# The output row of token 0 of a Fourier mixer: from a weighted row sum on VectorE to products with one stationary column, and a weight unit moved behind the copies

## The chip, the cores and the metric

The kernel runs on one core of a Trainium2 chip. A core has TensorE (PE, the matmul engine, with a loader for its stationary operand, PEld), VectorE (DVE), ScalarE (ACT), GpSimd (POOL) and SyncE (SP), each with a program of its own that it works through in order, and DMA engines that move data between memory and the core. The metric is the time of one execution on the device, in microseconds (us).

## The reference, cut to what matters

An encoder of two layers, for 512 tokens of 1024 channels. Layer 0 mixes with attention and a recurrent branch, layer 1 with a Fourier transform; after each mixer comes a SwiGLU FFN of 2816 hidden channels, and every part is normed before and after. The change is in the Fourier mixer:

```python
def fourier_mixer(h, w):
    B, S, D = h.shape
    g = h.astype(jnp.float32).reshape(B, S, FOURIER_GROUPS, FOURIER_GROUP_DIM)
    f = jnp.fft.fft2(g, axes=(1, 3), norm='ortho').real
    return f.reshape(B, S, D).astype(h.dtype) @ w

def reference(...):
    for l in range(DEPTH):
        hn = rmsnorm(x, ln_mix_pre[l])
        ...
            m = fourier_mixer(hn, w_fourier_out[l // 2])
        x = x + rmsnorm(m, ln_mix_post[l])
        hn = rmsnorm(x, ln_ffn_pre[l])
        x = x + rmsnorm(swiglu(hn, w_ffn_gate[l], w_ffn_up[l], w_ffn_down[l]), ln_ffn_post[l])
```

The real part of the transform is symmetric in the frequencies: it is the sum of a part E that is even and a part T that is odd, so two output rows come from one pair, as E + T and E − T.

## The kernel before, in words

**Products.** Each float32 operand is split into a high part and the rest (`split`: a cast on ACT at L104, a subtraction on DVE at L107), and `mm3` makes three products of the parts (L110 to L112).

**Weights.** They come in units of two halves of 512 KB. `prep_half` loads a half into one of three `raw` buffers (SP, L177 or L179), ACT makes `whi` of it and DVE `wlo`. A load has to wait until the `wlo` three halves earlier is done, and since ACT and DVE work in program order, the place where `prep_one` is called sets where the two halves stand in their queues. `next_unit` preps some units ahead; in the Fourier stage the calls of `prep_one` are written out by hand.

**The Fourier stage**, between the two FFNs. `pre_norm_tok` norms a token tile t into `hnhi` and `hnlo`. `pos_dft` and `pos_rest` transform over the positions (PE, out tile `put`; `take_u` splits it into `u`), `ch_dft` and `ch_rest` over the channels of each of the four groups g (out `pe` and `po`, split into `feo`). The linear map by w_fourier_out uses the folded weights `wfold` (sums and differences of rows j and 256 − j, written to memory by `fold_w` during the first FFN): `map_part(i, h, g)` accumulates, for 128 tokens i and 512 output channels h, the even part in `psm[i][0][h]` and the odd part T in `psm[i][1][h]`. The tile of tokens i=1 goes first. `map_rest` adds the rows that have no partner (channel 128 of each group, one more for the ends): `fr` with the weight tile `wr`.

**The row at token 0.** T is zero there, and its row in `psm[0][1][h]` takes the map of column 256 of the transforms instead, the partner of column 0. Before the change this row is summed on DVE: four `raw` loads of wfold (L1040), `acc` (L1042 to L1045) with the column values `e256` as scalars, split into `acch` and `accl`, and put into the row by two products with a one-hot column, L1064.

**Out of the map.** `map_out(i)` copies T to `yt` (ACT, L1070), makes the sum and the difference `y` (DVE, L1074), and norms: times gain (L297), sums of squares (ACT, L298), `m` and `r` (DVE L249 and L250, POOL L251), new `x` (L307), squares of x (ACT, L257), `xn` (L279). `turn_x` transposes xn on PE (`pT`, L287), ACT and DVE split it into `hnhi` and `hnlo` of the last FFN, whose first products are `pc` (L110 to L112 with 256 columns while only two tiles are there).

Of the kernel before, what the change touches and what calls it, by code (L numbers as in the profile page):

```python
# [10 lines left out]
F32 = mybir.dt.float32  # L11
F32R = mybir.dt.float32r
# [4 lines left out]
P = 128  # L17
D = 1024
# [17 lines left out]
def encoder_kernel(  # L36
# [27 lines left out]
    def tile1k(name, dtype=F32):  # L64
        return tiles.tile([P, 1024], dtype, name=nm(name), tag="t")
# [12 lines left out]
    def f(ap):  # L78
        return ap.bitcast(F32)
# [20 lines left out]

    def split(hi, lo, src, hi_eng=A, lo_eng=V):

        if hi_eng is A:
            A.copy(hi, src)  # L104
        else:
            hi_eng.tensor_copy(hi, src)
        lo_eng.tensor_tensor(out=lo, in0=src, in1=f(hi), op=ALU.subtract)  # L107

    def mm3(ps, l, r, start, stop, **kw):
        T.matmul(ps, lhsT=l[0], rhs=r[0], start=start, stop=False, **kw)  # L110
# [54 lines left out]
    emitted = [0]  # L165
    consumed = [0]

    def prep_half():
        i = emitted[0]
        if i >= len(units):  # L170
            return
        kind, ap = units[i]
        halves = prepped.setdefault(i, [])
        h = len(halves)
        raw = raws.tile([P, 1024], F32, name=nm("raw"), tag="raw")
        if kind == "c":
            nc.sync.dma_start(raw.rearrange("p (k c) -> p k c", c=256), ap[:, 4 * h:4 * h + 4, :])  # L177
        elif kind == "r":
            nc.sync.dma_start(raw, ap[:, h, :])  # L179
        else:  # L180
            nc.sync.dma_start(raw.rearrange("p (dh j) -> p dh j", j=P),
                              (lru_w_a, lru_w_i)[h].rearrange("d h i j -> i (d h) j"))
        hi, lo = tile1k("whi", F32R), tile1k("wlo", F32R)
        split(hi, lo, raw, hi_eng=V if i in HI_DVE else A, lo_eng=G if i in LO_POOL else V)
        halves.append((hi, lo))
        if h:
            emitted[0] += 1
# [13 lines left out]
    def fold_w(g):  # L201

        a, b, c = (tile1k("fold") for _ in range(3))
        nc.sync.dma_start(a, w_fourier_out[g * 256:g * 256 + P, :])
        gather(b, w_fourier_out, rowx["w%d" % g])
        G.memset(b[0:1, :], 0.0)
        V.tensor_tensor(out=c, in0=a, in1=b, op=ALU.add)
        V.tensor_tensor(out=a, in0=a, in1=b, op=ALU.subtract)
        for z, w in enumerate((c, a)):
            G.dma_start(wfold[g * 256 + z * P:g * 256 + (z + 1) * P, :], w)  # L210

    def prep_one():
        prep_half()
        prep_half()

    last_unit = [len(units)]

# [661 lines left out]
    def chw(i):  # L879
        return chT[i // 8][:, (i % 8) * P:(i % 8 + 1) * P]  # L880

    def load_ch():
        chT.extend(tile1k("ch", F32R) for _ in range(2))
        for z in range(2):
            for n in range(2):
                G.dma_start(chw(2 * z + n), dft_ch[n, :, z * 256:z * 256 + P])
        G.memset(f(chT[0][:, S:]), 0.0)
        G.memset(f(chT[1]), 0.0)
        for g in range(4):
            G.dma_start(chw(4 + g)[g:g + 1, :], dft_ch[0, 0:1, 512:512 + P])  # L890
# [3 lines left out]
        G.memset(f(chw(13)[:, 0:1]), 1.0)


    last_row = []

    def load_last():
        w128 = tile1k("w128")  # L900
        G.memset(w128, 0.0)
        for q in range(3):
            G.dma_start(w128[32 * q:32 * q + 4, :], w_fourier_out.rearrange("(g j) d -> g j d", j=256)[:, P, :])
        last_row.append(w128)

    posT = []
    calls = [0]
# [21 lines left out]
                posT[k].append(w)  # L929

    last_unit[0] = len(units) - 4 - NF // 2 * 3
    ffn(0, after0, 6, load_dft, early=lambda u: fold_w(u - 1) if 0 < u < 5 else None)
    last_unit[0] = len(units)
    load_last()
    prep_one()


# [37 lines left out]
        take_u(g)  # L975

    prep_one()
    w128, = last_row

    feo = hpool.tile([P, 16, 256], F32R, name=nm("feo"), tag="hnhi")  # L980
    rows_ = hpool.tile([P, 4, D], F32R, name=nm("rows"), tag="hnlo")
    acch, accl, wr, fr = rows_[:, 0, :], rows_[:, 1, :], rows_[:, 2, :], rows_[:, 3, 0:256]


    fe, fo, e256 = [None] * 4, [None] * 4, {}

    def ch_dft(g):
        pe, po = bank("pe"), bank("po")
        ut, ur = uts[g], uts["r"]
        mm3(pe[:, 0:258], (chw(0), chw(1)), [a[:, 0:258] for a in ut], True, False)  # L990
        for a in ur:
            T.matmul(pe[:, 0:258], lhsT=chw(4 + g)[0:4, :], rhs=a[0:4, 0:258], start=False, stop=a is ur[1])
        mm3(po[:, 0:256], (chw(2), chw(3)), [a[:, 256:512] for a in ut], True, True)
        eo = feo[:, 4 * g:4 * g + 4, :]
        e, o = fe[g], fo[g] = (eo[:, 0, :], eo[:, 1, :]), (eo[:, 2, :], eo[:, 3, :])
        split(*e, pe[:, 0:256])
        e256[g] = sm("e256")
        V.tensor_copy(e256[g], pe[:, 256:257])
        for a in o:
            G.memset(f(a[:, 0:1]), 0.0)  # L1000
        split(*[a[:, 1:256] for a in o], po[:, 1:256])

    def ch_rest():
        ps = bank("pe")
        n = 0
        for g in (0, 1, 2, 3, "r"):
            for a in uts[g]:
                k = 4 if g == "r" else P
                T.matmul(ps[:, 0:258], lhsT=chw(12 if g == "r" else 8 + g)[0:k, :], rhs=a[0:k, 0:258], start=n == 0, stop=n == 9)
                n += 1  # L1010
        e256["r"] = sm("e256")
        V.tensor_copy(e256["r"], ps[:, 256:257])
        c = A.copy(fr[:, 0:256], ps[:, 0:256])
        v = V.tensor_tensor(out=fr[64:P, 0:256], in0=ps[64:P, 0:256], in1=f(fr[64:P, 0:256]), op=ALU.subtract)
        order_after(A.copy(wr, w128), [c])
        order_after(V.tensor_tensor(out=wr[32:64, :], in0=w128[32:64, :], in1=f(wr[32:64, :]), op=ALU.subtract), [v])

    for g in range(4):
        ch_dft(g)
# [13 lines left out]
    wf = [next_unit(-1) for g in range(4)]  # L1033
    prep_one()


    acc = tile1k("acc")
    for g in range(4):
        raw = raws.tile([P, 1024], F32, name=nm("raw"), tag="raw")
        nc.sync.dma_start(raw, wfold[g * 256:g * 256 + P, :])  # L1040
        if g:
            V.scalar_tensor_tensor(out=acc, in0=raw, scalar=e256[g], in1=acc, op0=ALU.mult, op1=ALU.add)  # L1042
        else:
            V.tensor_scalar(out=acc, in0=raw, scalar1=e256[0], scalar2=None, op0=ALU.mult)
    V.scalar_tensor_tensor(out=acc[0:32, :], in0=w128[0:32, :], scalar=e256["r"][0:32, :], in1=acc[0:32, :], op0=ALU.mult, op1=ALU.add)  # L1045
    split(acch, accl, acc)
    prep_one()

    psm = [[[bank("pm"), bank("pm")] for _ in range(2)] for _ in range(2)]

    def map_part(i, h, g):
        sl = slice(i * P, (i + 1) * P)
        d = slice(h * S, (h + 1) * S)
        ps = psm[i]
        mm3(ps[0][h], [a[:, sl] for a in fe[g]], [a[:, d] for a in wf[g][0]], g == 0, False)
        mm3(ps[1][h], [a[:, sl] for a in fo[g]], [a[:, d] for a in wf[g][1]], g == 0, g == 3 and i == 1)

# [108 lines left out]
```

## Time and profile before

| what | value |
|---|---|
| median of 3 runs | 1036.85 us (1035.66 to 1037.36) |
| the profiled execution | 1037.44 us, span 1035.7 us, mean granted clock 0.984 |
| PE busy | 1001.8 us (97% of the span) |
| DVE busy | 500.7 us (48%) |
| ACT busy | 377.9 us (36%) |
| POOL busy | 115.4 us (11%) |

Times in the trace count from the start of the span; the Fourier stage lies from about 594 to 655 us. The busy share of PE is a mean over the whole program, and where a short stretch has another limit it does not show there. Idle time of an engine matters only if the work that ends last waits for it.

### The profile page before, as it was taken

The numbers are of one execution on the slowest core, as the hardware profiler recorded it, in microseconds if no ns is written. First come the engines' busy times: TensorE is split into PE (matmuls) and PEld (weight loads), VectorE is DVE, ScalarE is ACT, GpSimd is POOL, SyncE is SP. The second block draws the span as 40 slices with busy tenths as digits, with TensorE's granted clock in tenths as the row PEclk, the third lists the DMA queues.
The fourth block names the chain that finished last, engine by engine and source line by source line (L and its number), as shares of the span: only waits on it lengthen the run. The fifth ranks groups of instructions, "written<-read, shape, count | busy, mean of one in ns | idle before, by whom it ended". The sixth has DMA issues, their size and how long they took to land.

```text
span 1035.7 us, 12334 instructions
## 1 busy us (share of the span) xinstructions
PE 1001.8 (97%) x4877; PEld 835.4 (81%) x4877; DVE 500.7 (48%) x765; ACT 377.9 (36%) x621; POOL 115.4 (11%) x196
## 2 busy tenths in 40 slices
PE   8999999999999999999999997699999999999996
PEld 7887677789888888888888886698888888888885
DVE  6869988753554222223323688726422232343304
ACT  5378567643333211232213464515311322233201
POOL 1056111111020000005130130100000000000001
PEclk8999999999999999999999999799999999999998
DMA  6424212412776432223442067017622233124002
GB/s 219 130 84 142 93 41 82 144 40 83 240 271 204 136 104 82 82 82 79 136 122 82 3 212 235 21 42 220 186 82 82 81 120 104 61 95 129 1 1 81
DMA packets 79797, 114.78 MB, mean 111 GB/s; under 512 B 6466, under 2 KB 66415, under 8 KB 79740
## 3 DMA queue, kind: packets, MB, share of 16 engines
q1 hardware_dynamic: 70858, 97.16, 29.7%
q0 software_dynamic: 8592, 16.32, 5.2%
q8 instruction: 38, 0.62, 0.3%
q10 hardware_dynamic: 290, 0.53, 0.1%
q14 instruction: 19, 0.16, 0.0%
HBM read 106.65 MB, written 7.34 MB: 110 GB/s over the span
## 4 chain that ended last, share of the span: by engine, by line
PE 82%; DVE 9%; issue 3%; DMA 2%; ACT 2%; POOL 1%; SPq 0%; DVEq 0%; POOLq 0%; ACTq 0%
PE pc L112 15%; PE pc L111 15%; PE pc L110 15%; PE pj L112 9%; PE pj L111 9%; PE pj L110 9%; DVE wlo L107 2%; DVE p L630 2%; DVE p L636 1%; DMA raw<-wfold 1%; PE pT L287 1%; DMA raw<-in_w_in_dram 1%; DVE aT L107 1%; PE pqk L110 1%; ACT whi L104 1%
## 5 line engine op out<-in xcount | busy, mean ns | idle before, releaser
L107 DVE TENSOR_TENSOR wlo<-raw,whi 128x1024 fp32r<-128x1024 f32 x170 | 207.0, 1239 | 206.7 <-ACT whi L104 173.8
L112 PE MATMUL pc<-hnhi,wlo 128*128 128x512 f32 (+1 forms) x784 | 288.2, 368 | 2.6 <-DVE wlo L107 2.6
L111 PE MATMUL pc<-hnlo,whi 128*128 128x512 f32 (+1 forms) x784 | 288.5, 369 | 0.0
L110 PE MATMUL pc<-hnhi,whi 128*128 128x512 f32 (+1 forms) x784 | 287.4, 369 | 1.1 <-ACT whi L104 0.6
L104 ACT CAST whi<-raw 128x1024 fp32r<-128x1024 f32 x164 | 167.9, 1049 | 108.7 <-DMA raw<-in_w_ffn_gate_dram 47.6
L112 PEld LDWEIGHTS pc<-hnhi,wlo 128*128 128x128 f32 x784 | 148.5, 189 | 27.2 <-DVE wlo L107 3.1
L110 PEld LDWEIGHTS pc<-hnhi,whi 128*128 128x128 f32 x784 | 147.7, 189 | 26.4 <-ACT hnhi L104 1.2
L111 PEld LDWEIGHTS pc<-hnlo,whi 128*128 128x128 f32 x784 | 148.6, 189 | 24.7 <-DVE hnlo L107 0.4
L110 PE MATMUL pj<-whi,gs 128*128 128x512 f32 x352 | 136.9, 389 | 0.0
L112 PE MATMUL pj<-whi,gs 128*128 128x512 f32 x352 | 136.9, 389 | 0.0
L111 PE MATMUL pj<-wlo,gs 128*128 128x512 f32 x352 | 136.9, 389 | 0.0
L94 ACT ACTIVATE gated<-pc 128x512 f32<-128x512 f32 x44 | 26.1, 597 | 242.8 <-PE pc L112 242.8
L797 DVE TENSOR_TENSOR gated<-gated,pc 128x512 f32<-128x512 f32 x44 | 30.1, 686 | 111.9 <-PE pc L112 111.7
L112 PEld LDWEIGHTS pj<-whi,gs 128*128 128x128 f32 x352 | 66.1, 188 | 13.8
L110 PEld LDWEIGHTS pj<-whi,gs 128*128 128x128 f32 x352 | 66.1, 188 | 13.8
L111 PEld LDWEIGHTS pj<-wlo,gs 128*128 128x128 f32 x352 | 66.1, 188 | 13.5
L251 POOL TENSOR_TENSOR r<-m,mhalf 128x1 f32<-128x1 f32 x32 | 19.2, 599 | 497.4 <-DVE m L250 456.1
L107 DVE TENSOR_TENSOR gs<-gated,gs 128x512 fp32r<-128x512 f32 x44 | 28.8, 688 | 74.7 <-ACT gs L104 74.6
L104 ACT CAST gs<-gated 128x512 fp32r<-128x512 f32 x44 | 25.5, 619 | 100.5 <-PE pj L111 53.2
L298 ACT ACTIVATE junk<-pj 128x512 f32<-128x512 f32 x24 | 14.3, 597 | 75.0 <-DVE y L297 53.9
L297 DVE TENSOR_TENSOR y<-pj,gpost 128x512 f32<-128x512 f32 x24 | 16.4, 686 | 48.7 <-PE pj L112 48.7
L94 ACT ACTIVATE p<-p,mn 128x512 f32<-128x512 f32 x32 | 23.0, 719 | 25.8 <-DVE mn L630 24.3
(255 smaller groups left out, 1217.1 us busy)
## 6 DMA issues: line engine op xcount, KB each, us to landing
raw<-in_w_ffn_gate_dram SPq DMA_DIRECT2D x44, 512.0 KB, 4.2
raw<-in_w_ffn_up_dram SPq DMA_DIRECT2D x44, 512.0 KB, 4.9
raw<-in_w_ffn_down_dram SPq DMA_DIRECT2D x44, 512.0 KB, 3.4
raw<-in_w_in_dram SPq DMA_DIRECT2D x20, 512.0 KB, 4.4
raw<-wfold SPq DMA_DIRECT2D x12, 512.0 KB, 4.4
raw<-in_w_mix_out_dram SPq DMA_DIRECT2D x8, 512.0 KB, 3.4
wfold<-fold POOLq DMA_DIRECT2D x8, 512.0 KB, 3.3
fold<-in_w_fourier_out_dram SPq DMA_DIRECT2D x4, 512.0 KB, 6.7
```

The lines of the kernel that those rows point to most:

```text
L94: ins = A.activation(out_, in_, func, **kw)
L104: A.copy(hi, src)
L107: lo_eng.tensor_tensor(out=lo, in0=src, in1=f(hi), op=ALU.subtract)
L110: T.matmul(ps, lhsT=l[0], rhs=r[0], start=start, stop=False, **kw)
L111: T.matmul(ps, lhsT=l[0], rhs=r[1], start=False, stop=False, **kw)
L112: T.matmul(ps, lhsT=l[1], rhs=r[0], start=False, stop=stop, **kw)
L251: G.tensor_tensor(out=r, in0=m, in1=mhalf[:, 0:1], op=ALU.pow)
L287: T.transpose(pt[:, k * P:(k + 1) * P], xh[:, k * P:(k + 1) * P], ident)
L297: V.tensor_tensor(out=ys[h], in0=ps[h], in1=g[:, h * S:(h + 1) * S], op=ALU.mult)
L298: sq[0] = A.activation(junk, ps[h], AF.Square, scale=RD, accum_out=ss[h])
L630: last_score[0] = V.tensor_tensor_reduce(out=pr[m], in0=ps[m], in1=bias[h][:, 384 - t * P:384 - t * P + S], op0=ALU.add, op1=ALU.min, scal ...
L797: V.tensor_tensor(out=gated[fc], in0=gated[fc], in1=ps, op=ALU.mult)
```

## The change

In the Fourier stage, the row at token 0 is made on PE: `map_row(h)` accumulates into partition 0 of `psm[0][1][h]` 13 products with one stationary column (the column 256 of the transforms, held as high and low part in `ends`, four columns for the four groups, and one column of `fr`), each with 512 moving columns. The DVE sum `acc`, its four loads, its split and the L1064 products go. The weight tile `wr` is made by `fold_last` in the first FFN (u=5), written to memory as `wlast` and loaded once by POOL. `prep_one` of the second unit moves from before the map into `map_out(1)`, behind the copies of T, and its casts are ordered after the last copy.

```diff
     def split(hi, lo, src, hi_eng=A, lo_eng=V):
 
-        if hi_eng is A:
-            A.copy(hi, src)
-        else:
-            hi_eng.tensor_copy(hi, src)
+        c = A.copy(hi, src) if hi_eng is A else hi_eng.tensor_copy(hi, src)
         lo_eng.tensor_tensor(out=lo, in0=src, in1=f(hi), op=ALU.subtract)
+        return c
...
-        split(hi, lo, raw, hi_eng=V if i in HI_DVE else A, lo_eng=G if i in LO_POOL else V)
+        order_after(split(hi, lo, raw, hi_eng=V if i in HI_DVE else A, lo_eng=G if i in LO_POOL else V), after)
...
+    def fold_last():
+
+        a, b = tile1k("fold"), tile1k("fold", F32R)
+        G.memset(a, 0.0)
+        for q in range(3):
+            nc.sync.dma_start(a[32 * q:32 * q + 4, :], w_fourier_out.rearrange("(g j) d -> g j d", j=256)[:, P, :])
+        A.copy(b, a)
+        V.tensor_tensor(out=b[32:64, :], in0=a[32:64, :], in1=f(b[32:64, :]), op=ALU.subtract)
+        G.dma_start(wlast, f(b))
...
-    ffn(0, after0, 6, load_dft, early=lambda u: fold_w(u - 1) if 0 < u < 5 else None)
+    ffn(0, after0, 6, load_dft, early=lambda u: fold_w(u - 1) if 0 < u < 5 else fold_last() if u == 5 else None)
     last_unit[0] = len(units)
-    load_last()
     prep_one()
...
-    acch, accl, wr, fr = rows_[:, 0, :], rows_[:, 1, :], rows_[:, 2, :], rows_[:, 3, 0:256]
+    wr, fr = rows_[:, 0, :], rows_[:, 1, 0:258]
+
+    ends = rows_[:, 2, 0:4], rows_[:, 2, 4:8]
+    G.dma_start(f(wr), wlast)
...
-        e256[g] = sm("e256")
-        V.tensor_copy(e256[g], pe[:, 256:257])
+        split(*[a[:, g:g + 1] for a in ends], pe[:, 256:257])
...
-    prep_one()
-
-
-    acc = tile1k("acc")
-    for g in range(4):
-        raw = raws.tile([P, 1024], F32, name=nm("raw"), tag="raw")
-        nc.sync.dma_start(raw, wfold[g * 256:g * 256 + P, :])
...
-    split(acch, accl, acc)
     prep_one()
...
         T.matmul(psm[i][0][h], lhsT=fr[:, sl], rhs=wr[:, d], start=False, stop=True)
-        if i == 0:
-            for a in (acch, accl):
-                T.matmul(psm[i][1][h], lhsT=chw(13), rhs=a[:, d], start=False, stop=a is accl)
+
+    def map_row(h):
+
+        d = slice(h * S, (h + 1) * S)
+        row = psm[0][1][h][0:1, :]
+        T.matmul(row, lhsT=fr[:, 256:257], rhs=wr[:, d], start=False, stop=False)
+        for g in range(4):
+            mm3(row, [a[:, g:g + 1] for a in ends], [a[:, d] for a in wf[g][0]], False, False)
...
         for h in range(2):
-            A.copy(ts[h], psm[i][1][h])
+            copied[0] = A.copy(ts[h], psm[i][1][h])
...
+        if i:
+            prep_one(copied)
...
+                if g == 3 and i == 0:
+                    map_row(h)
                 map_part(i, h, g)
```

The lines of the changed kernel lie elsewhere (a cast of `split` is L103, its subtraction L104, mm3 L108 to L110, the y of map_out L1060). DVE in the map, before: `acc` is the row sum, the `rows` tile its low part, and the two `wlo` around it those of the second unit (up).

```order
L107 TENSOR_TENSOR wlo_5214<-raw_5211,whi_5213 128x1024
L1044 TENSOR_SCALAR acc_5217<-raw_5218,e_839_5098 128x1024
L1042 SCALAR_TENSOR_TENSOR acc_5217<-raw_5221,e_842_5116,acc_5217 128x1024
L1042 SCALAR_TENSOR_TENSOR acc_5217<-raw_5224,e_845_5134,acc_5217 128x1024
L1042 SCALAR_TENSOR_TENSOR acc_5217<-raw_5227,e_848_5152,acc_5217 128x1024
L1045 SCALAR_TENSOR_TENSOR acc_5217<-w_810_4925,e_850_5169,acc_5217 32x1024
L107 TENSOR_TENSOR wlo_5236<-raw_5233,whi_5235 128x1024
L107 TENSOR_TENSOR rows_5085<-acc_5217,rows_5085 128x1024
L107 TENSOR_TENSOR wlo_5242<-raw_5239,whi_5241 128x1024
L1074 TENSOR_TENSOR y_5304<-pm_5249,yt_5303 128x512
L1074 TENSOR_TENSOR y_5304<-pm_5250,yt_5303 128x512
L297 TENSOR_TENSOR y_5309<-y_5304,gpost_5177 128x512 x2
```

The same place in the changed kernel, from the first y on (the row ahead of it is the wlo of the second gate half):

```order
L1060 TENSOR_TENSOR y_5277<-pm_5222,yt_5276 128x512
L1060 TENSOR_TENSOR y_5277<-pm_5223,yt_5276 128x512
L306 TENSOR_TENSOR y_5282<-y_5277,gpost_5178 128x512 x2
L1060 TENSOR_TENSOR yt_5276<-pm_5222,yt_5276 128x512
L1060 TENSOR_TENSOR yt_5276<-pm_5223,yt_5276 128x512
L306 TENSOR_TENSOR y_5291<-yt_5276,gpost_5178 128x512 x2
L104 TENSOR_TENSOR wlo_5301<-raw_5298,whi_5300 128x1024
L258 TENSOR_SCALAR m_5310<-ss_5283 128x1
L259 TENSOR_TENSOR m_5311<-ss_5284,m_5310 128x1
L258 TENSOR_SCALAR m_5318<-ss_5292 128x1
L104 TENSOR_TENSOR wlo_5307<-raw_5304,whi_5306 128x1024
L316 SCALAR_TENSOR_TENSOR x_82<-y_5282,r_5312,x_82 128x512 x2
```

The five acc rows and the split of acc are gone, and the two wlo of up stand now behind the y products, one ahead of the `m` and one ahead of the first `x`.

DVE at the end of the norm of token tile 3, before (`w` is the folded input; `hnlo` the low part that the transform over positions reads; the two wlo are the halves of the first wfold unit):

```order
L853 TENSOR_TENSOR w_4916<-h_4914 128x4x127
L854 TENSOR_TENSOR w_4916<-h_4914 128x4x127
L107 TENSOR_TENSOR wlo_4933<-raw_4930,whi_4932 128x1024
L860 SCALAR_TENSOR_TENSOR hnlo_4689<-w_4916,r_4910,hnhi_4688 128x512 x2
L107 TENSOR_TENSOR wlo_4939<-raw_4936,whi_4938 128x1024
L107 TENSOR_TENSOR u_5033<-put_5020,u_5033 4x258
```

and after:

```order
L862 TENSOR_TENSOR w_4925<-h_4923 128x4x127
L863 TENSOR_TENSOR w_4925<-h_4923 128x4x127
L104 TENSOR_TENSOR wlo_4937<-raw_4934,whi_4936 128x1024
L104 TENSOR_TENSOR wlo_4943<-raw_4940,whi_4942 128x1024
L869 SCALAR_TENSOR_TENSOR hnlo_4698<-w_4925,r_4919,hnhi_4697 128x512 x2
L104 TENSOR_TENSOR u_5037<-put_5024,u_5037 4x258
```

The second wlo stands ahead of the hnlo pair instead of behind it.

PE at the last group of the map for i=0 in the changed kernel (`pm` are the accumulators, `rows` the stationary columns of `ends` or `fr`, `feo` the transform of the tokens):

```order
L108 MATMUL pm_5221<-whi_5190,feo_5088 128x512
L109 MATMUL pm_5221<-wlo_5191,feo_5088 128x512
L110 MATMUL pm_5221<-whi_5190,feo_5088 128x512
L1048 MATMUL pm_5220<-rows_5089 1x512
L108 MATMUL pm_5220<-whi_4936,rows_5089 1x512
L109 MATMUL pm_5220<-wlo_4937,rows_5089 1x512
L110 MATMUL pm_5220<-whi_4936,rows_5089 1x512
L108 MATMUL pm_5220<-whi_5078,rows_5089 1x512
L109 MATMUL pm_5220<-wlo_5079,rows_5089 1x512
L110 MATMUL pm_5220<-whi_5078,rows_5089 1x512
```

Before, none of the 1x512 rows is there, and the map ends with these:

```order
L110 MATMUL pm_5248<-whi_5201,feo_5084 128x512
L111 MATMUL pm_5248<-wlo_5202,feo_5084 128x512
L112 MATMUL pm_5248<-whi_5201,feo_5084 128x512
L1061 MATMUL pm_5245<-rows_5085 128x512
L1064 MATMUL pm_5247<-rows_5085,ch_4063 128x512 x2
L1061 MATMUL pm_5246<-rows_5085 128x512
L1064 MATMUL pm_5248<-rows_5085,ch_4063 128x512 x2
L287 MATMUL pT_5423<-ident,xn_5341 128x128 x4
```

Thirteen products with one stationary column come ahead of the last group of each h, and the pairs of L1064 go.

## Rows read from the trace of the kernel before

**Rows 1.** Waits of PE: engine, line, releaser; us in total, times, longest.

```profile
PE pT L287 <- ACT yt L1070: 11.7, 1, 11.7
...
PE pc L112 <- DVE wlo L107: 2.6, 1, 2.6
```

**Rows 2.** The chain that ended last, 605 to 690 us: start, us, what.

```profile
630.60 3.17 DMA raw<-wfold
633.86 1.29 DVE acc L1042
635.17 4.63 DMA raw<-in_w_ffn_up_dram
```

**Rows 3.** Timeline of PE: start, us, line, out<-in, stationary shape, output, count [idle before].

```profile
606.84 0.28 PE L110 MATMUL put<-pos,hnhi 128*4 128x258 f32 x1
...
608.01 0.28 PE L111 MATMUL put<-pos,hnhi 128*4 128x258 f32 x1
...
608.37 0.28 PE L112 MATMUL put<-pos,hnlo 128*128 128x258 f32 x1
```

**Rows 4.** Timeline of DVE at the same place.

```profile
607.02 1.41 DVE L860 SCALAR_TENSOR_TENSOR hnlo<-w,r,hnhi 128x512 fp32r<-128x512 f32 x2
608.57 1.23 DVE L107 TENSOR_TENSOR wlo<-raw,whi 128x1024 fp32r<-128x1024 f32 x1
```

**Rows 5.** Timeline of PE, the map of i=0 and the transposes.

```profile
629.52 0.39 PE L110 MATMUL pm<-whi,feo 128*128 128x512 f32 x1
...
640.18 0.39 PE L112 MATMUL pm<-whi,feo 128*128 128x512 f32 x1
...
641.31 0.61 PE L1064 MATMUL pm<-rows,ch 128*128 128x512 f32 x2
653.60 1.94 PE L287 MATMUL pT<-ident,xn 128*128 128x128 f32 x8 [11.67 <-ACT yt L1070]
```

**Rows 6.** Timeline of DVE, from the last gate half to the next unit.

```profile
629.35 1.23 DVE L107 TENSOR_TENSOR wlo<-raw,whi 128x1024 fp32r<-128x1024 f32 x1 [1.74 <-ACT whi L104]
...
642.25 1.29 DVE L1074 TENSOR_TENSOR y<-pm,yt 128x512 f32<-128x512 f32 x2
...
648.15 1.41 DVE L307 SCALAR_TENSOR_TENSOR x<-y,r,x 128x512 f32<-128x512 f32 x2 [0.62 <-POOL r L251]
...
656.44 1.94 DVE L107 TENSOR_TENSOR hnlo<-pT,hnhi 128x512 fp32r<-128x512 f32 x3
658.52 0.69 DVE L107 TENSOR_TENSOR hnlo<-pT,hnhi 128x512 fp32r<-128x512 f32 x1 [0.15 <-ACT hnhi L104]
...
659.73 1.28 DVE L297 TENSOR_TENSOR y<-y,gpost 128x512 f32<-128x512 f32 x2
...
673.23 2.36 DVE L107 TENSOR_TENSOR wlo<-raw,whi 128x1024 fp32r<-128x1024 f32 x2
```

**Rows 7.** Timeline of ACT: a weight cast, the copies of i=0, the hnhi casts.

```profile
607.50 1.04 ACT L104 CAST whi<-raw 128x1024 fp32r<-128x1024 f32 x1
...
652.43 1.05 ACT L1070 COPY yt<-pm 128x512 f32<-128x512 f32 x2
...
657.91 0.58 ACT L104 CAST hnhi<-pT 128x512 fp32r<-128x512 f32 x1 [0.26 <-PE pT L287]
...
671.54 1.07 ACT L104 CAST hnhi<-pT 128x512 fp32r<-128x512 f32 x2 [0.32 <-PE pT L287]
```

**Rows 8.** Timeline of PE in the last FFN: the later transposes, the wait for wlo.

```profile
670.90 1.04 PE L287 MATMUL pT<-ident,xn 128*128 128x128 f32 x8
674.51 0.39 PE L112 MATMUL pc<-hnhi,wlo 128*128 128x256 f32 x1 [2.57 <-DVE wlo L107]
```

**Rows 9.** Busy time by stretch: PE, PEld, DVE, ACT, POOL, PE clock, DMA share, GB/s.

```profile
350.00:420.00 70.00, 70.00 (x311) 57.98 (x310) 18.29 (x18) 16.54 (x20) 0.00 (x0) 1.00 0.30 90
...
670.00:674.50 4.50, 1.62 (x12) 1.38 (x12) 3.73 (x8) 2.29 (x4) 0.55 (x1) 1.00 0.00 0
674.50:678.50 4.00, 3.99 (x20) 3.99 (x21) 2.29 (x3) 0.00 (x0) 0.00 (x0) 0.57 0.70 196
```

More of the change, by code (lines that the diff above doesn't have):

```diff
@@ L159, in encoder_kernel @@
     wfold = dram.tile([D, D], F32, name="wfold")
+    wlast = dram.tile([P, D], F32, name="wlast")
     for u in range(4):
@@ L166, in encoder_kernel, with prep_half @@
     consumed = [0]
-    def prep_half():
+    def prep_half(after=()):
         i = emitted[0]
@@ L210, in fold_w, with prep_one @@
             G.dma_start(wfold[g * 256 + z * P:g * 256 + (z + 1) * P, :], w)
-    def prep_one():
-        prep_half()
-        prep_half()
+    def fold_last():
[6 more added lines that the diff above has]
+        G.dma_start(wlast, f(b))
+    def prep_one(after=()):
+        prep_half(after)
+        prep_half(after)
     last_unit = [len(units)]
@@ L893, in load_ch @@
             G.dma_start(chw(12)[g:g + 1, g:g + 65:32], dft_ch[0, 0:1, 0:3])
[L894 to L904, printed above, removed]
     posT = []
@@ L977, in encoder_kernel @@
     prep_one()
-    w128, = last_row
     feo = hpool.tile([P, 16, 256], F32R, name=nm("feo"), tag="hnhi")
     rows_ = hpool.tile([P, 4, D], F32R, name=nm("rows"), tag="hnlo")
-    acch, accl, wr, fr = rows_[:, 0, :], rows_[:, 1, :], rows_[:, 2, :], rows_[:, 3, 0:256]
-    fe, fo, e256 = [None] * 4, [None] * 4, {}
+    wr, fr = rows_[:, 0, :], rows_[:, 1, 0:258]
+    ends = rows_[:, 2, 0:4], rows_[:, 2, 4:8]
+    G.dma_start(f(wr), wlast)
+    fe, fo = [None] * 4, [None] * 4
     def ch_dft(g):
@@ L1010, in ch_rest @@
                 n += 1
[L1011 to L1016, printed above, removed]
+        A.copy(fr, ps[:, 0:258])
+        V.tensor_tensor(out=fr[64:P, :], in0=ps[64:P, 0:258], in1=f(fr[64:P, :]), op=ALU.subtract)
     for g in range(4):
@@ L1034, in encoder_kernel @@
     prep_one()
-    acc = tile1k("acc")
-    for g in range(4):
-        raw = raws.tile([P, 1024], F32, name=nm("raw"), tag="raw")
-        nc.sync.dma_start(raw, wfold[g * 256:g * 256 + P, :])
[L1041 to L1045, printed above, removed]
-    split(acch, accl, acc)
-    prep_one()
     psm = [[[bank("pm"), bank("pm")] for _ in range(2)] for _ in range(2)]
@@ L1055, in map_part @@
         mm3(ps[0][h], [a[:, sl] for a in fe[g]], [a[:, d] for a in wf[g][0]], g == 0, False)
-        mm3(ps[1][h], [a[:, sl] for a in fo[g]], [a[:, d] for a in wf[g][1]], g == 0, g == 3 and i == 1)
+        mm3(ps[1][h], [a[:, sl] for a in fo[g]], [a[:, d] for a in wf[g][1]], g == 0, g == 3)
     def map_rest(i, h):
@@ L1080, in map_out @@
             pre_norm(t, g_fpre1, after=sq[0])
+    copied = [None]
     for i in (1, 0):
```

## The prediction, made before the changed kernel ran

> **What bounds the kernel now.** I read the waits of TensorE (PE) first, because nothing can be gained where PE never waits. After the start of the program there is one long entry: the transposes pT at L287, the first work of the last FFN, wait 11.7 us, put down to ACT's yt at L1070. Behind it stand 2.6 us of pc L112 on a wlo of VectorE (DVE) [rows 1]. Everything the change touches lies just in front of these.
>
> The chain of waits says who is late. Around 631 to 641 us it does not run over PE: it goes over a load of wfold for acc, over the DVE product acc, and over a load of the up unit that could start only behind it [rows 2]. PE's own timeline shows the map meanwhile running without a gap: its part for i=0 starts at 629.52, the 48 products of 512 columns are spaced (640.18 − 629.52)/47 = 0.227 us, the last pair begins at 641.31, and PE then stands still until 653.60 [rows 5]. The copies of i=1 could have been made soon after 629.5, when PE had left that part. But DVE works in program order: the y of map_out(1) starts at 642.25, because acc, its splits and two wlo stand ahead of it in DVE's queue [rows 6]. From that y to the last xn are 14.2 us (642.25 to 656.44, where the hnlo that follows it begins) [rows 6], and they are the wait of PE. So the bound of this stretch is DVE's queue, not PE, and the reader should see that a kernel which is busy on PE nearly everywhere has here a place where PE work can be added and DVE work taken away at a profit.
>
> **The change, part by part.**
>
> *The row sum leaves DVE.* Four loads, acc, its two halves and the wr cast go. The y of map_out(1) then waits for two things only: the wlo ahead of it, and the copies of i=1. That wlo (second gate half) ends at 629.35 + 1.23 = 630.6 now [rows 6]; the side cost below moves it by about 1.1 us, to 631.7. PE ends i=1 at 629.5 + 1.1 = 630.6, and the two copies (1.05 us for both, from the pair of i=0 [rows 7]) end at about 631.8. So y starts near 631.7, 10.5 us earlier.
>
> *Two wlo move into map_out(1).* The second unit (up, two halves) is now split behind the copies of T, and DVE has one wlo ahead of the m's and one ahead of x. Each is 1.23 us. The second falls in the 0.62 us that x waits for POOL today [rows 6], so together they lengthen the chain by 1.2 + 0.6 = 1.8 us. The last xn is ready 14.2 + 1.8 = 16.0 us after y: 631.7 + 16.0 = 647.7. The two loads behind it need a raw buffer that a wlo of the last wfold unit sets free; the load of up in the chain took 4.63 us [rows 2]. By the same distance they land near 633, and DVE reaches the first wlo only four pairs of products after y, some 1.2 us each (1.29 with the tail of the second [rows 6]), at 636.5. That is the cover; if the load came later than about 635.6 (one cast of 1.04 us earlier [rows 7]), each us would lengthen the chain by one.
>
> *PE gets the row.* It is 26 products with one stationary column and 512 moving ones, and the four of L1064 go. No row has one stationary column with 512 moving ones. The nearest have 4 columns and 258: (608.01 − 606.84)/10 = 0.117 us each, against (608.37 − 608.01)/3 = 0.120 us with 128 columns [rows 3]. So the number of stationary columns does not matter there and I take the 0.227 us of the map: 26 × 0.227 = 5.9 us, less 4 × 0.227 = 0.9. As bounds, 0.217 us (the ratio 0.117/0.120), and 0.39 us, the duration of one map product [rows 5], if each had to end before the next: 5.6 and 10.1 us. The Trainium skill (TensorE: Matmul & The Clock Gate, "Back-to-back issue gap") gives about 0.131 us for each of a sustained stream of 512 columns, and 26 × 0.131 would be 3.4 us. The map's rows show 0.227, so its figure is not in the sum; by it PE would be done 2.5 us earlier, DVE's last xn would hold the transposes, and the gain would be 1.2 us larger (1027.6).
>
> *The side cost at the transforms.* On DVE the hnlo pair of token tile 3 now stands behind a second wlo, and on PE the last product of 4x258 with that hnlo stands two places earlier, ahead of every other use of the tile. Now the pair starts at 607.02 and PE reaches its hnlo at 608.37 without a wait [rows 3, 4]. With one wlo of 1.23 us first, from 606.9, the pair of 1.41 us ends at about 609.5, so PE waits some 1.1 us (bounds 0 and 1.23). Its raw data are there: ACT's cast for it at 607.50 waits for nothing but its turn [rows 7]. The whole of PE's later work, and with it the y above, moves by 1.1.
>
> *What costs nothing.* The fold of the last rows moves into the first FFN: one cast of ACT, a subtraction on 32 rows, three small loads on SP and two POOL items. There PE is busy 70.0 of 70 us while ACT has 16.5 and DVE 18.3 [rows 9]; without that cover it would be a cast of about 1.0 and a subtraction of about 1.2 us, and ACT standing some 4.6 us for a load. The wr load on POOL (512 KB) is issued during the transforms and first read at the end of i=1, just before 630.6; a load of that size took 4.63 us [rows 2]. The eight column splits take the place of five copies and a cast. The third part of wfold may be late by 0 to 0.6 us for the last map group, since two wlo moved behind the 64x258 subtraction; I leave it out of the sum and in the range.
>
> *The sum.* PE's map now ends at 641.31 + 2 × 0.227 = 641.76. After: 641.76 + 1.1 + 5.9 − 0.9 = 647.8, which I call E. It nearly coincides with the last xn at 647.7, so the transposes hardly wait. Behind E the yt copies on ACT end at E + 1.2 (1.05 us and a little for the signal). Four hnhi follow, 1.07 − 0.58 = 0.49 us apart, so the last begins at E + 2.7; its hnlo comes 0.61 us later (657.91 to 658.52) and the first y L297 another 0.6 later, E + 3.9 = 651.7 [rows 6, 7]. The transposes do not delay this: eight at the high clock are 1.04 us, not the 1.94 us of those that follow the long wait [rows 5, 8]. Before, y L297 began at 659.73 [rows 6], so it comes 8.0 us earlier. From y L297 the DVE chain is the same as before down to the wlo pair at 673.23, and it is this pair for which PE waits at 674.51 [rows 6, 8]. PE comes to that point earlier by nearly the same, since its first products pc follow the same hnlo, so the wait of 2.57 us stays about as long and everything behind it moves by 8.0. The profiled execution took 1037.44 us with a span of 1035.7; 1037.44 − 8.0 = 1029.4. It lies 0.6 us above the median of 1036.85, so the median should be **1028.8 us**.
>
> **Rivals.**
>
> *The clock does not fall at 674.* After the 2.57 us wait the granted clock is 0.57 over 4 us [rows 9]: the lower of 1.2 and 2.4 GHz for (1 − 0.57)/0.5 = 0.86 of it, which costs half of 3.4 us, 1.7 us less a little at the edges, 1.6. Before that stretch PE had an 11.7 us rest and a low clock; afterwards it comes from unbroken work, but the rest just before (1.62 of 4.5 us busy now) stays, so the fall may come again or not. Without it: 1027.2. The skill (same page, "Part 1") says the level falls after idle time and that the place varies from run to run, which fits either case. Chance 0.22.
>
> *Weights come late.* If loads land later than I think, for instance because the 512 KB of wr share the DMA with wfold, y or x slips. From the last xn to that y L297 are 2.8 us (transposes 1.04, two hnhi, one hnlo), against 3.9 from E, so 1.1 us of slip is free and each further us costs one. With the up load as late as now, 635.17 + 4.63 = 639.8 [rows 2], xn would end near 639.8 + 1.0 + 1.2 + 8.3 = 650.4 and the gain be 6.5; with 3 to 5 us of delay it is 4 to 6: 1031 to 1033. Against it: DMA has four loads fewer here. Chance 0.2.
>
> *The wait is only replaced.* The 2.57 us wait could grow by what PE gains, if the wlo of 673.23 were held by something other than DVE's chain, such as its load: then nothing is gained, 1036.9. The rows show DVE busy in a chain until that wlo with its casts long done, so 0.06.
>
> *Slower.* The row products run one after another in a single output row. If they cannot overlap, and the clock is low meanwhile, each could cost 2 × 0.39 = 0.78 us, 20.3 us together, 14.4 more than in the sum: 1028.8 + 14.4 = 1043.2. It decides from 26 × (c − 0.227) = 8.0, or c = 0.53 us a product. Against it: the map runs at the high clock without a gap until then, and accumulating into one bank costs nothing there [rows 5]. Chance 0.05.
>
> **How the numbers follow.** The forecast, a gain of 8.0 give or take 1.3, has 0.47. Its own range is 1027.5 to 1030.1. With the rival without the fall of the clock below and most of late weights above, the range is 1026.2 to 1033.2, and what it leaves out (0.06, 0.05 and some tail of late weights) is under 2 in 10. A measurement of this kernel can tell about 0.2% (2.1 us) from no change. Faster: 0.47 + 0.22 + 0.2 = 0.89; the same 0.06; slower 0.05.
>
> **What would show it.** In the profile after, the pT wait on yt should be gone; the first y of map_out(1) should start near 632; 26 row products should be spaced 0.227 us and the map end near 648; a new wait of about 1 us should stand in front of the 4x258 product with hnlo; the wlo wait at pc L112 (its line is L110 then) should stay between 2 and 3 us. I am wrong if row products take more than 0.3 us each, if y starts after 634, or if the wlo wait grows to 5 us or more.

## The result, and the profile after

The changed kernel takes 1028.26 us (median of 4 runs, 1027.21 to 1029.4); the kernel before, run in turn with it, 1036.39 us (4 runs, 1035.66 to 1037.36). The ratio is 0.9925 with an interval of 0.9913 to 0.9938, so 8.1 us are gained (by the interval 6.4 to 9.0). Run again beside later experiments it gave 1028.89 us against 1036.59, ratio 0.9934 (0.992 to 0.9947). The profiled execution took 1028.54 us with a span of 1026.8 us, 8.9 us under that of before.

Not all of the 8.9 us belong to the change. The PE row that stood at 608.01 [rows 3] stands at 606.74 after, 1.27 us earlier. Two stretches of both traces show where it comes from (start and end, length, busy time of PE, PEld, DVE, ACT and POOL with counts, PE clock, DMA share, GB/s). First before, then after:

```profile
10.00:20.00 10.00, 9.35 (x47) 7.93 (x48) 7.52 (x15) 7.10 (x15) 1.10 (x2) 0.70 0.72 244
...
180.00:190.00 10.00, 7.84 (x38) 6.45 (x37) 8.99 (x17) 9.52 (x18) 1.01 (x1) 0.83 0.65 184
```

```profile
10.00:20.00 10.00, 9.32 (x54) 7.87 (x53) 7.80 (x15) 8.00 (x17) 1.10 (x2) 1.00 0.65 216
...
180.00:190.00 10.00, 7.58 (x44) 6.07 (x43) 8.98 (x17) 9.51 (x17) 1.01 (x1) 1.00 0.66 198
```

From 10 to 20 us the granted clock was 0.70 in the one and 1.00 in the other, from 180 to 190 us 0.83 and 1.00. Behind the first stretch the same cast of ACT stands at 25.97 and 25.50, 0.47 us apart; behind the second the same row of ACT stands at 217.96 and 216.67, 1.29 us apart, and up to the stage the distance hardly changes. In the profiles of the experiments the clock was anything from 0.70 to 1.00 from 10 to 20 us. So every place below is compared from a marker just ahead of the stage, and 1.27 us are added to times of after to read them against before.

The waits of PE after the change, from 560 to 700 us (engine, line, releaser; us in total, times, longest):

```profile
PE pc L110 <- DVE wlo L104: 2.6, 1, 2.6
PE put L110 <- DVE hnlo L869: 0.9, 1, 0.9
PE pc L108 <- ACT hnhi L103: 0.6, 2, 0.3
```

The 11.7 us of [rows 1] are gone, and the transposes pT wait for nothing there; 0.6 us on hnhi stand behind them, a new 0.9 us at the transforms, and the wait for wlo as before. PE's timeline shows the four places:

```profile
606.74 0.28 PE L109 MATMUL put<-pos,hnhi 128*4 128x258 f32 x1
...
608.20 0.40 PE L110 MATMUL put<-pos,hnlo 128*4 128x258 f32 x2 [0.95 <-DVE hnlo L869]
...
641.80 0.40 PE L1048 MATMUL pm<-rows 128*1 128x512 f32 x1
...
644.56 0.39 PE L110 MATMUL pm<-whi,rows 128*1 128x512 f32 x1
...
646.15 0.62 PE L1042 MATMUL pm<-rows 128*128 128x512 f32 x2
...
665.70 0.39 PE L110 MATMUL pc<-hnhi,wlo 128*128 128x256 f32 x1 [2.58 <-DVE wlo L104]
```

The 13 row products of the second half are spaced (644.56 − 641.80)/12 = 0.230 us, and the map ends at 646.15 + 2 × 0.227 = 646.6, without a gap. DVE's timeline of the same stretch:

```profile
606.74 1.41 DVE L869 SCALAR_TENSOR_TENSOR hnlo<-w,r,hnhi 128x512 fp32r<-128x512 f32 x2
...
630.85 1.29 DVE L1060 TENSOR_TENSOR y<-pm,yt 128x512 f32<-128x512 f32 x2
...
637.30 1.23 DVE L104 TENSOR_TENSOR wlo<-raw,whi 128x1024 fp32r<-128x1024 f32 x1
638.99 1.42 DVE L316 SCALAR_TENSOR_TENSOR x<-y,r,x 128x512 f32<-128x512 f32 x2 [0.46 <-POOL r L260]
...
646.01 1.42 DVE L288 SCALAR_TENSOR_TENSOR xn<-x,r,gpre 128x512 f32<-128x512 f32 x2 [0.66 <-POOL r L260]
647.34 1.28 DVE L1060 TENSOR_TENSOR y<-pm,yt 128x512 f32<-128x512 f32 x2
648.54 2.48 DVE L104 TENSOR_TENSOR hnlo<-pT,hnhi 128x512 fp32r<-128x512 f32 x4
650.93 1.28 DVE L306 TENSOR_TENSOR y<-y,gpost 128x512 f32<-128x512 f32 x2
```

The y of map_out(1), at 642.25 before [rows 6], starts at 630.85. The last four rows follow each other without idle time. This is also what the chain of waits names there (start, us, what):

```profile
646.01 0.59 DVE xn L288
...
647.34 1.28 DVE y L1060 x2
648.63 2.39 DVE hnlo L104 x4
651.02 1.20 DVE y L306 x2
```

From y L306 (L297 before) the stretch up to the wait for wlo is as it was: 650.93 against 659.73 [rows 6] is 8.80 us earlier, 665.70 against 674.51 [rows 8] is 8.81. Less the 1.27 us from ahead of the stage, the change itself gives 7.5 us in the trace.

### The profile page after: what moved, and what is told of

Its sections match the earlier page's. It is cut to its first block, busy times and chain, and to the rows that moved or that the text cites. A ratio compares the mean times of both kernels' runs of the same rounds, so it can differ in the third digit from the quotient of the medians.

```text
span 1026.8 us, 12365 instructions
## 1 busy us (share of the span) xinstructions
PE 1004.6 (98%) x4899; PEld 834.5 (81%) x4899; DVE 493.9 (48%) x758; ACT 377.2 (37%) x624; POOL 116.2 (11%) x194
## 4 chain that ended last, share of the span: by engine, by line
PE 78%; DVE 12%; issue 3%; ACT 2%; DMA 2%; POOL 1%; SPq 0%; DVEq 0%; POOLq 0%; ACTq 0%
PE pc L110 15%; PE pc L108 15%; PE pc L109 15%; PE pj L110 8%; PE pj L109 8%; PE pj L108 8%; DVE wlo L104 2%; DVE p L639 2%; DVE p L645 1%; DVE y L306 1%; DVE x L316 1%; DMA raw<-in_w_in_dram 1%; POOL r L260 1%; DVE aT L104 1%; PE pqk L108 1%
## 5 line engine op out<-in xcount | busy, mean ns | idle before, releaser
L104 DVE TENSOR_TENSOR wlo<-raw,whi 128x1024 fp32r<-128x1024 f32 x170 | 207.0, 1240 | 199.0 <-ACT whi L103 166.1
L110 PE MATMUL pc<-hnhi,wlo 128*128 128x512 f32 (+1 forms) x784 | 288.3, 369 | 2.6 <-DVE wlo L104 2.6
L108 PE MATMUL pc<-hnhi,whi 128*128 128x512 f32 (+1 forms) x784 | 287.7, 369 | 1.0 <-ACT hnhi L103 0.8
L103 ACT CAST whi<-raw 128x1024 fp32r<-128x1024 f32 x164 | 167.9, 1049 | 107.3 <-DMA raw<-in_w_ffn_gate_dram 49.9
L110 PEld LDWEIGHTS pc<-hnhi,wlo 128*128 128x128 f32 x784 | 148.4, 189 | 27.4 <-DVE wlo L104 3.1
L108 PEld LDWEIGHTS pc<-hnhi,whi 128*128 128x128 f32 x784 | 147.9, 189 | 26.3 <-ACT hnhi L103 1.5
L108 PE MATMUL pj<-whi,gs 128*128 128x512 f32 x352 | 136.9, 389 | 0.0
L110 PE MATMUL pj<-whi,gs 128*128 128x512 f32 x352 | 136.9, 389 | 0.0
L108 PEld LDWEIGHTS pj<-whi,gs 128*128 128x128 f32 x352 | 66.1, 188 | 13.8
L110 PEld LDWEIGHTS pj<-whi,gs 128*128 128x128 f32 x352 | 66.1, 188 | 13.7
L104 DVE TENSOR_TENSOR gs<-gated,gs 128x512 fp32r<-128x512 f32 x44 | 28.8, 687 | 74.7 <-ACT gs L103 74.6
L103 ACT CAST gs<-gated 128x512 fp32r<-128x512 f32 x44 | 25.5, 619 | 100.5 <-PE pj L109 53.2
L306 DVE TENSOR_TENSOR y<-pj,gpost 128x512 f32<-128x512 f32 x24 | 16.4, 688 | 48.7 <-PE pj L110 48.7
```

Of the source, the lines that this page charges most:

```text
L103: c = A.copy(hi, src) if hi_eng is A else hi_eng.tensor_copy(hi, src)
L110: T.matmul(ps, lhsT=l[1], rhs=r[0], start=False, stop=stop, **kw)
L306: V.tensor_tensor(out=ys[h], in0=ps[h], in1=g[:, h * S:(h + 1) * S], op=ALU.mult)
```

## The experiments

Each is timed in turn with the kernel before. hnlo L869 at 606.74 of after is the marker by which places in kernels that keep its two wlo ahead of it are compared.

**The row alone.** The changed kernel with the second unit put back ahead of the map:

```diff
     last_unit[0] = len(units)
     prep_one()
...
+    prep_one()
...
-        if i:
-            prep_one(copied)
```

> The changed kernel with its second unit (up) split ahead of the map again, so that both its wlo stand in front of the first y on DVE. The theory is that the chain on DVE from the first y of map_out(1) to the y L297 of i=0 sets the time: the second up half is issued at 629.4 and lands near 633.5, so its wlo ends near 636.3 instead of 630.85, and the chain behind it has two wlo fewer (1.8 us): 3.4 to 3.7 us slower than the changed kernel, some 1031.8 us. The rival, that only the end of the map on PE (E) counts and the place of the unit is free: no difference, 1028.3.

Measured: 1031.02 us against 1035.89, ratio 0.9945 (0.9931 to 0.9959). DVE's timeline of this kernel:

```profile
636.49 1.23 DVE L104 TENSOR_TENSOR wlo<-raw,whi 128x1024 fp32r<-128x1024 f32 x1 [1.37 <-ACT whi L103]
637.75 1.29 DVE L1061 TENSOR_TENSOR y<-pm,yt 128x512 f32<-128x512 f32 x2
...
655.60 1.28 DVE L306 TENSOR_TENSOR y<-y,gpost 128x512 f32<-128x512 f32 x2
```

The intervals of this kernel and the changed one (0.9913 to 0.9938) overlap at their ends; the trace tells the two apart: y waits for the weights again and starts 637.75 − 630.85 less the marker's 1.33 = 5.6 us later than in the changed kernel, and y L306 comes 655.60 − 650.93 less 1.33 = 3.34 us later. The move is worth that much in the stage, nearly what was expected (3.4 to 3.7). Of the span (1030.0 against 1026.8 us) only 3.2 − 1.33 = 1.9 us are left of it. The clock falls in the changed kernel behind the wait for wlo (the row is shown below); in this kernel's windows, where its wait of 1.1 us ends at 670.4, it does not:

```profile
668.00:676.00 8.00, 6.90 (x59) 6.66 (x58) 4.65 (x6) 1.07 (x2) 0.00 (x0) 1.00 0.40 131
```

That fits the 1.5 us between 3.34 and 1.9.

**The move alone.** The kernel before, its row sum on DVE kept, with the second unit behind the copies:

```diff
-    prep_one()
...
+        if i:
+            prep_one(copied)
```

> The kernel before with the second unit behind the copies and nothing else: acc, its four loads and the L1064 products stay, and its DVE rows now stand among the y of map_out(1). The theory of the DVE queue: what held the y was the wlo of up and the split of acc, so the y starts near 632 and only the up loads, still behind those of acc (landing 637 and 639.8), hold the chain: last xn near 650.4 against 656.4, and 6 to 6.5 us faster than before, 1030.2 us. The rival, that the row sum itself was the cost and must leave DVE for any gain: about the time of before, 1035 to 1037.

Measured: 1033.25 us against 1035.89, ratio 0.9976 (0.9965 to 0.9987): a gain of 2.6 us, less than expected. DVE's timeline shows why:

```profile
630.64 0.69 DVE L1071 TENSOR_TENSOR y<-pm,yt 128x512 f32<-128x512 f32 x1
631.25 1.28 DVE L1040 SCALAR_TENSOR_TENSOR acc<-raw,e,acc 128x1024 f32<-128x1024 f32 x1
...
640.76 0.68 DVE L295 TENSOR_TENSOR y<-yt,gpost 128x512 f32<-128x512 f32 x1
641.37 2.34 DVE L104 TENSOR_TENSOR wlo<-raw,whi 128x1024 fp32r<-128x1024 f32 x2
```

The first y starts as early as in the changed kernel, but acc stands between its pieces, and DVE works on both without a gap until the m's at 643.64. So acc costs not only by its place ahead of y but by its own work, on a DVE that has no time to spare there: this other order does not do, and the gain of the change came when the work left. Orders that keep acc and put it behind the y were not tried. The two parts alone gave 4.9 and 2.6 us, together 7.5, near the whole; since the clock has a share of some 1.5 us in the 4.9, the sum is no proof that the parts are independent.

**No row products.** The changed kernel without map_row (the row of T at token 0 is left out):

```diff
-                if g == 3 and i == 0:
-                    map_row(h)
```

> The changed kernel without the 26 row products (the row at token 0 is left out of T). By the DVE theory PE's end of the map has only some 0.4 us on the path, since DVE reaches the y of i=0 at 647.34 with yt done at 646.9: 0 to 0.7 us faster than the changed kernel, 1027.6 to 1028.3. By the rival, that PE is the bound of this stretch again, 26 x 0.227 = 5.9 us faster, 1022.4.

Measured: 1027.53 us against 1035.89, ratio 0.9918 (0.9904 to 0.9932), which overlaps the interval of the changed kernel. PE now waits, and for the same xn:

```profile
645.68 1.94 PE L296 MATMUL pT<-ident,xn 128*128 128x128 f32 x8 [4.12 <-DVE xn L288]
```

DVE's timeline has y L306 here:

```profile
651.83 1.28 DVE L306 TENSOR_TENSOR y<-y,gpost 128x512 f32<-128x512 f32 x2
```

With the marker at 607.47 that is 0.2 us later than in the changed kernel. Taking 26 × 0.230 = 6.0 us of PE work away moves nothing forward: the products lie in time in which PE would wait for DVE. The span still ends 1.3 us earlier (1026.2 against 1026.8, and 0.73 of the marker), and what differs is the clock, which does not fall behind the wait for wlo in this kernel: it is 1.00 from 666 to 674 us.

**The row products twice.** map_row called twice in a row (the row then counts double):

```diff
                 if g == 3 and i == 0:
                     map_row(h)
+                    map_row(h)
```

> The changed kernel with the 26 row products issued twice (the row at token 0 is doubled). The map on PE ends 5.9 us later, at 652.5, and the yt copies with it, where DVE has 0.4 us to spare: 5.5 us slower than the changed kernel, 1033.7, still faster than before. If the row products hid behind DVE with room to spare: no difference, 1028.3.

Measured: 1032.74 us against 1035.89, ratio 0.9969 (0.9957 to 0.9981). PE's timeline at the end of the map, then DVE's:

```profile
651.98 0.62 PE L1042 MATMUL pm<-rows 128*128 128x512 f32 x2
```

```profile
652.48 1.29 DVE L1060 TENSOR_TENSOR y<-pm,yt 128x512 f32<-128x512 f32 x2 [5.37 <-PE pm L1042]
...
656.10 1.28 DVE L306 TENSOR_TENSOR y<-y,gpost 128x512 f32<-128x512 f32 x2
```

Another 26 products, 26 × 0.230 = 6.0 us, push y L306 back by 5.4 us (marker 606.51). So the cover that the 26 products of the changed kernel have is used up but for some 0.6 us: PE and DVE end there almost together. Of the 5.4 us the span shows 3.9; the clock did not fall in this kernel.

**The fold alone.** The kernel before with fold_last added to its first FFN:

```diff
-... fold_w(u - 1) if 0 < u < 5 else None)
+... fold_w(u - 1) if 0 < u < 5 else fold_last() if u == 5 else None)
```

> The kernel before with fold_last added in the first FFN and nothing else (its result is written to memory and not read). If PE there has the cover that the prediction gave it, no difference to the kernel before, 1036 us. The rival, that ACT stands for the small loads long enough to make a weight cast late: 1 to 5 us slower.

Measured: 1036.31 us against 1036.63, ratio 0.9995 (0.9986 to 1.0004). It costs nothing that can be measured.

**hnlo ahead of the second wlo.** The changed kernel, with the second wlo at the transforms ordered after the hnlo pair of token tile 3:

```diff
-    prep_one()
+    prep_half()
+    prep_half((), last_lo)
```

> The changed kernel with the hnlo pair of token tile 3 ordered ahead of the second wlo again, as before the change. The wait of 0.95 us in front of the product with hnlo goes. If it is on the path (the end of the map, the loads behind the wlo and the DVE chain all follow the transforms), 0.9 us faster than the changed kernel, 1027.3. The rival: the DVE chain starts with the landing of the second gate half and does not follow, no difference, 1028.2.

Measured: 1027.78 us against 1036.63, ratio 0.9913 (0.99 to 0.9927). The wait of 0.95 us on PE has shrunk to 0.2, but y starts hardly earlier:

```profile
629.48 1.23 DVE L104 TENSOR_TENSOR wlo<-raw,whi 128x1024 fp32r<-128x1024 f32 x1 [0.30 <-ACT whi L103]
630.74 1.29 DVE L1062 TENSOR_TENSOR y<-pm,yt 128x512 f32<-128x512 f32 x2
```

With the first wlo of the pair as marker (604.74 against 604.47 in the changed kernel), y starts 0.38 us earlier, not 0.95, right behind the wlo of the second gate half. The span is as much earlier (1026.7 against 1026.8, and 0.27 of the marker). So 0.4 of the 0.95 us reach the end, and not all of the stall as the sum had it; the measured time cannot be told from that of the changed kernel.

**The wait for wlo at pc L110.** Three attempts on what the change leaves. First, the next unit's splits ahead of the y of map_out(0), behind the pre-norm of map_out(1) (`prep_one()` after that loop); then the same with the two splits on POOL (`LO_POOL = (54,)`):

> The changed kernel with the third unit (gate, two halves) split behind the norms of map_out(1) and no longer behind those of map_out(0). The wait of 2.6 us for its wlo goes, and with it the low clock behind it (1.5 us in the profile). But its two wlo, 2.4 us, now stand ahead of the y of i=0 on DVE, which works without a gap there, so y L306 comes 2.4 us later and the transposes of the other tiles with it: 0.2 to 1.7 us faster than the changed kernel, 1026.5 to 1028. The rival, that the DVE chain has room for two wlo: 4 us faster, 1024.2.

> As the run with the third unit behind the norms of map_out(1), but its low halves are made on POOL, which has 9 us without work there. The wait of 2.6 us and the low clock behind it go and the DVE chain keeps its place: 2.6 to 4.1 us faster than the changed kernel, 1024.1 to 1025.6. The rival, that POOL's passes slow DVE's or come late for the r of the norms: no gain, 1028 or more.

Measured: 1030.25 and 1031.31 us against 1036.63, ratios 0.9938 (0.9925 to 0.9952) and 0.995 (0.9936 to 0.9963); both expectations were missed, and of the second its rival came about. In the first, DVE does the pair at once, and PE waits for what stands behind it:

```profile
647.43 2.35 DVE L104 TENSOR_TENSOR wlo<-raw,whi 128x1024 fp32r<-128x1024 f32 x2
```

```profile
651.63 0.39 PE L108 MATMUL pc<-hnhi,whi 128*128 128x256 f32 x1 [2.29 <-DVE hnlo L104]
```

The wait of 2.58 us is replaced by one of 2.29. In the second, DVE's last xn pair stretches from 1.42 to 5.59 us while POOL splits (DVE's timeline, then POOL's):

```profile
647.01 5.59 DVE L288 SCALAR_TENSOR_TENSOR xn<-x,r,gpre 128x512 f32<-128x512 f32 x2 [0.66 <-POOL r L260]
```

```profile
646.94 5.11 POOL L104 TENSOR_TENSOR wlo<-raw,whi 128x1024 fp32r<-128x1024 f32 x2
```

Third, the unit is prepared behind the copies in both calls of map_out, each half in a place where the norm waits:

```diff
-        if i:
-            prep_one(copied)
+        prep_one(copied)
```

> The changed kernel with the third unit (gate) also behind the copies of T, those of map_out(0): its two wlo then stand ahead of the first m and ahead of the first x of that half, where DVE waits 1.1 us for POOL's r, and not behind the last xn. They are done near 657, before PE needs them at 662, so the 2.6 us wait and the low clock behind it go; about 1 us comes back where the four transposes' hnlo are made in one piece: 1.7 to 3.4 us faster than the changed kernel, 1024.9 to 1026.5. The rival, from the run with this unit behind the norms of map_out(1): the wait is only replaced by one of the same size, 1028 to 1030.

Measured: 1025.34 us (1025.16 to 1025.66) against 1036.59, ratio 0.9896 (0.9881 to 0.9911), beside 1028.89 us for the changed kernel run in turn with it: 3.5 us better than the change, 11.3 better than before. In the profiled executions it is 2.5 us (spans 1023.9 and 1026.8, less 0.4 of the marker, which stands at 606.33). Its waits of PE from 630 to 700 us, and the windows of this kernel:

```profile
PE pT L296 <- DVE hnlo L104: 1.0, 1, 1.0
PE pc L108 <- DVE hnlo L104: 0.8, 2, 0.6
PE pc L109 <- DVE hnlo L104: 0.2, 1, 0.2
```

```profile
640.00:680.00 40.00, 37.88 (x279) 33.55 (x279) 24.18 (x46) 16.90 (x38) 5.43 (x8) 1.00 0.19 56
```

No wait for wlo is left, the waits that stand there come to 2.0 us, and the clock stays at 1.00.

**Both.** The last one together with hnlo ahead of the second wlo:

> As the run with the third unit behind the copies of map_out(0), and the hnlo pair of token tile 3 ahead of the second wlo as well. If the two are independent, another 0.4 us: 1024.5 to 1026. If what the second gains is lost again behind the first, no difference to it.

Measured: 1025.13 us (1024.51 to 1025.74) against 1036.59, ratio 0.9896 (0.9881 to 0.9911), not to be told from the third attempt alone, though the span of its profiled execution is 1.2 us shorter (1022.7 against 1023.9).

**The changed kernel again**, run in turn with these two:

> The changed kernel once more, beside the two runs that change it: 1028.3 us, 0.9925 of the time before. Whether the clock falls again behind the 2.6 us wait is open; with the fall the profile is 1.5 us longer than without.

Measured: 1028.89 us (1028.03 to 1029.79), as given above. In this second profile of it the clock falls again behind the wait for wlo:

```profile
666.00:670.00 4.00, 4.00 (x24) 4.00 (x23) 1.43 (x3) 0.00 (x0) 0.00 (x0) 0.57 0.87 257
```

## Why the prediction held, step by step

Times of after are given with the 1.27 us added.

- *The bound is DVE's queue.* Shown. The row products can be taken away without a gain (4.12 us of wait come back), while either half of the relief of DVE gives time by itself.
- *y starts at 631.7.* It came at 630.85 + 1.27 = 632.1, but for another reason than the one given, so that the nearness is luck. It follows the wlo of the second gate half, and that wlo starts at 629.60 + 1.27 = 630.9, 1.5 us later than before [rows 6]. The side stall was 0.95 us, not 1.1, and without it this start is only 0.38 us earlier. The other 1.1 us come with the load of that half. The chains of waits have it, before and after:

```profile
624.39 3.78 DMA raw<-in_w_ffn_gate_dram
```

```profile
623.35 5.06 DMA raw<-in_w_ffn_gate_dram
```

  The load sets out at nearly the same time (623.35 + 1.27 = 624.6) and takes 1.28 us more. Why it takes longer stays open.
- *Two wlo lengthen the chain from y to the last xn by 1.8 us, to 16.0.* It became 647.34 − 630.85 = 16.5. **This term was too small by 0.5 us.** The second wlo was to fall in the 0.62 us in which x waits for POOL's r [rows 6], and did not. POOL's timeline after, with the r that x waits for first:

```profile
637.37 1.58 POOL L260 TENSOR_TENSOR r<-m,mhalf 128x1 f32<-128x1 f32 x1 [25.32 <-DVE m L258]
640.62 0.55 POOL L260 TENSOR_TENSOR r<-m,mhalf 128x1 f32<-128x1 f32 x1 [1.67 <-ACT xn L266]
```

  The r that lies beside the wlo of 637.30 took 1.58 us instead of 0.55, and ended 0.42 us behind that wlo (638.95 and 638.53). The cover was itself made longer by what it was to cover.
- *26 products at 0.227 us.* They take 0.230, and the map ends at 646.6 + 1.27 = 647.9 (forecast 647.8; its terms add up to 647.9). The rival of products that run one after another is refuted, as is the shorter sum by the figure of the Trainium skill (TensorE: Matmul & The Clock Gate, "Back-to-back issue gap") that the prediction weighed: 0.230 us is nowhere near 0.131.
- *From the last xn to y L297 2.8 us, so that E + 3.9 decides and xn may slip 1.1 us.* **This is the step that failed.** It takes 650.93 − 647.34 = 3.6 us, because DVE has the y pair of map_out(0) to do between xn and the hnlo (1.20 us and 2.39 us in the chain above). Before, one y of that pair stood ahead of the last xn and the other behind the hnlo:

```profile
654.36 0.69 DVE L1074 TENSOR_TENSOR y<-pm,yt 128x512 f32<-128x512 f32 x1
...
659.13 0.68 DVE L1074 TENSOR_TENSOR y<-pm,yt 128x512 f32<-128x512 f32 x1
```

  The 2.8 us had room for neither; even before, the way was 659.73 − 656.44 = 3.3 us [rows 6]. The way from E is the shorter one: with the row twice, where PE holds the y, the map ends at 651.98 + 2 × 0.227 = 652.4 and y L306 starts 3.7 us later. By that it would have come at 646.6 + 3.7 = 650.3 in the changed kernel; it came at 650.93. So DVE's chain ends last, by 0.6 us, and the 0.5 us lost on the way to xn went straight into the result. The runs without the row and with it twice bear that out from both sides: 0.2 us and 5.4 of 6.0.
- *y L297 at 651.7.* It came at 652.2; the gain in the stage is 7.5 and not 8.0 us. That the medians gave 8.1 us, nearer to the forecast than the trace, is luck: their interval of 6.4 to 9.0 us does not tell 7.5 from 8.0.
- *The wait for wlo stays, and the clock falls behind it.* Both did: 2.58 us, and in the windows of after

```profile
666.00:670.00 4.00, 4.00 (x23) 4.00 (x22) 1.98 (x3) 0.00 (x0) 0.00 (x0) 0.57 0.76 227
```

  (1 − 0.57)/0.5 × 4 = 3.4 us at the lower of the levels 1.2 and 2.4 GHz, as before the change [rows 9]. The rival without this fall came about in neither profile of the changed kernel.
- *The fold costs nothing.* Shown by itself.
- *Late weights.* In a small way they came about: the load of the second gate half cost y some 1.1 us, as said above, where the rival had 3 to 5. (In that rival 639.8 + 1.0 + 1.2 + 8.3 is 650.3 and not 650.4.) The up loads did not hold the chain: ahead of the wlo at 637.30 there is no idle time.
- *A wait only replaced.* It did not come about: the wait for wlo stayed at 2.58 us.

## What to carry to other kernels

Where an engine works in program order, ask first what stands ahead of the operation that others wait for, and whether the engine has slack at all: another order on the same engine brought a third of the gain, and the rest came only when the work went to an engine that would have waited there. When two chains are forecast to end within 1 us of each other, work both out instruction by instruction, since the cover of the one is a term of the other. After such a change look for the next wait on the same engine: here one condition less put the next unit's splits into waits of the norm and gave 3.5 us more, while the same splits one place earlier, ahead of the y of map_out(0), only exchanged one wait for another.

## What the runs showed of the hardware

An operation of POOL and one of DVE that reads two tensors can stop each other, which I had not expected. A 128x1 operation of POOL took 1.58 us beside a DVE subtraction and 0.55 where DVE stood idle for it; a DVE pair took 5.59 us beside two subtractions of POOL and 1.42 in the changed kernel. The Trainium skill (SBUF — State Buffer, "SBUF: two separate sides") says that a DVE operation with two inputs in SBUF and a GpSimd operation that reads SBUF share a port pair, which the one that starts first holds for its whole instruction while the other stands; both cases agree with it.

The clock behind a short wait is not settled. The windows with twice the row products, 4.5 us up to the end of the same wait of 2.58 us and the 8 us that follow:

```profile
666.40:670.90 4.50, 1.93 (x18) 1.69 (x16) 3.73 (x8) 2.25 (x4) 0.55 (x1) 1.00 0.00 0
...
672.00:680.00 8.00, 7.76 (x65) 7.52 (x64) 2.43 (x4) 1.07 (x2) 0.00 (x0) 1.00 0.40 130
```

The changed kernel, with nearly the same busy time just ahead:

```profile
661.20:665.70 4.50, 1.92 (x18) 1.68 (x17) 3.73 (x8) 2.28 (x4) 0.55 (x1) 1.00 0.02 4
```

fell to 0.57 behind it, in both of its profiles; this one did not fall. By the spans the fall costs some 1.5 us: 3.34 against 1.9 us for the row alone, 5.4 against 3.9 for the row twice (3.9 is 1030.5 − 1026.8 and 0.23 of the marker), 0.2 later against 1.3 earlier without the row. What decides it stays open; that it is more than the wait itself is what these two kernels show.
